# Half of the attention heads scored with keys on partitions, in a two-layer hybrid decoder trunk

## The chip, the cores and the metric

The kernel runs on one core of one Trainium2 chip. A core has five engines that work side by side, each through its own instructions in order: TensorE (PE, matrix products into PSUM; its weight loads are listed as PEld), VectorE (DVE), ScalarE (ACT), GpSimd (POOL) and SyncE (SP, here the queue of the loads). The metric is the device time of one execution in microseconds (us); less is better.

## The reference, cut to what matters

Two layers work on 256 positions of width 1024. Each has a feed-forward part, a mixer and a second feed-forward part. With 256 positions and key blocks of 256 there is one block, so the attention of the mixer is plain causal attention of 8 heads of 64:

```python
def hybrid_layer(x, ...):
    x = x + 0.5 * swiglu(rms_norm(x, ffn1_norm), ffn1_w_gate_up, ffn1_w_down)
    h = rms_norm(x, mix_norm)
    z = h @ w_in                       # u, q, k, v and the gates' inputs gl
    y_pool = multiscale_pool(u, pool_w, pool_scale)
    q = rope(rms_norm(q per head, q_norm)); k = rope(rms_norm(k per head, k_norm))
    # per head: s = q k^T / 8, masked where key > query; p = softmax(s); y = p v
    y_attn = moba_attention(q, k, v)
    gates = sigmoid(gl + b_gate)
    merged = gates[0] * (y_pool @ w_branch_pool) + gates[1] * (y_attn @ w_branch_attn)
    x = x + merged @ w_out
    x = x + 0.5 * swiglu(rms_norm(x, ffn2_norm), ffn2_w_gate_up, ffn2_w_down)
    return x
```

Everything is float32 in and out.

## The kernel before

**Layout.** Activations are held transposed: features on the 128 partitions, the 256 positions in the free dimension. Each float32 operand of a large product is split into two parts (`hi` and `lo`, type fp32r), and a product is three partial products: hi times hi, hi times lo, lo times hi. `chain` (through `prod`, line 118) does the first two in one matmul of 512 columns and the third in one of 256.

**Weights.** They arrive in units of 128 x 2048 values, each loaded by SP into one of 4 `raw` buffers and split in halves: ACT rounds a half to `hi` (line 103), DVE subtracts to get `lo` (line 104). There are 6 buffers `hl` for split halves, so a half can be split as soon as PE has finished with the one six halves earlier. `ask` keeps two units ahead.

**Order.** PE's order is the order in which the program is written. Those of DVE and ACT are laid down at build time by a scheduling planner, which goes by the program's order and by its own estimates of durations; on the chip each engine then keeps to that fixed order, and an instruction that waits holds up everything behind it on its engine. `tc.issue_after` pins a few instructions behind others.

**The mixer**, one call of `mix` per layer, in PE's order: the products `tokens` for q, k and v (positions on partitions), the product for u, the transposes of q and k to features on partitions (`to_features`, line 437), `gate(0)`, scores of heads 0 to 3, gates 1 and 2, transposes of their probabilities (`by_key`, line 472), gate 3, their values (line 481), then scores of heads 4 to 7 (line 446), gates 4 and 5, the pool map, gate 6, `by_key` for heads 4 to 7, gate 7, their values; then the two branch products with `pk` and `yk`, merged with the gates, and the product with `w_out`. A pair `p` is heads 2p and 2p + 1.

**Softmax before.** `scores` puts queries on partitions and keys in the free dimension. `softmax` adds the mask and takes the largest score of each row in one DVE instruction (line 457), ACT takes the exponential with the row's sum as a by-product (line 462), with the norm factor `fq` of the query as its per-partition scale; DVE divides (lines 464 and 466). `by_key` then transposes three 128 x 128 blocks of probabilities per head on PE into PSUM and ACT copies them out (line 474), since the product with v needs the keys on partitions. `halves` splits the result into `yk` (lines 179 and 180).

**PSUM.** The pool `pmm` has two buffers of two banks (gates, k, u, branches), the pool `pat` four buffers of one bank. A gate product needs the `pmm` buffer of the gate before the last one; `drain` (lines 175 and 176) empties it with an ACT copy and a DVE addition. The branch products use the same two buffers and the merge (lines 605 to 614) empties them.

**GpSimd** does small copies inside `pool` (line 500) and, in `reduced` (line 243), one sum over partitions of a 128 x 256 tile ahead of most of the norms.

Of the kernel before, what the change touches and what calls it, by code (L numbers as in the profile page):

```python
# [11 lines left out]
F32 = mybir.dt.float32  # L12
F32R = mybir.dt.float32r
AF = mybir.ActivationFunctionType
OP = mybir.AluOpType
# [3 lines left out]
P = 128  # L19
D = 1024  # L20
S = 256
# [4 lines left out]
NH = 8  # L26
DH = 64
GW = 512
# [4 lines left out]
NEG = -1e30  # L33
# [7 lines left out]
def trunk_kernel(ctx: ExitStack, tc: tile.TileContext, x_in, w_in, pw_in, qkn_in, rope_in, mask_in, band_in, out):  # L41
    nc = tc.nc
    ctx.enter_context(nc.allow_low_precision("float32r parts of exactly split float32 operands"))
    const = ctx.enter_context(tc.tile_pool(name="const", bufs=1))
    raws = ctx.enter_context(tc.tile_pool(name="raws", bufs=4))
    parts = ctx.enter_context(tc.tile_pool(name="parts", bufs=6))
    acts = ctx.enter_context(tc.tile_pool(name="acts", bufs=1))
    tmp = ctx.enter_context(tc.tile_pool(name="tmp", bufs=2))
    small = ctx.enter_context(tc.tile_pool(name="small", bufs=4))
    pmm = ctx.enter_context(tc.tile_pool(name="pmm", bufs=2, space=PSUM))  # L50
    pat = ctx.enter_context(tc.tile_pool(name="pat", bufs=4, space=PSUM))
# [3 lines left out]
    act = nc.scalar.activation  # L55
    tt = nc.vector.tensor_tensor
    stt = nc.vector.scalar_tensor_tensor
    mm = nc.tensor.matmul
# [119 lines left out]
    def halves(d, v):  # L178
        act(d[:, 0, :], v, AF.Copy)  # L179
        tt(d[:, 1, :], v, d[:, 0, :].bitcast(F32), op=OP.subtract)  # L180
# [15 lines left out]
    make_identity(nc, ident)  # L196
    mask = const.tile([P, 3, P], F32, name="mask")
    nc.gpsimd.memset(mask[:, 0, :], 0.0)
    rope = const.tile([P, 2, 2, DH], F32, name="rope")
    cnt = const.tile([P, 16], F32, name="cnt")  # L200

# [2 lines left out]
    acc = acts.tile([P, S], F32, name="acc")  # L204
# [18 lines left out]
    def rsqrt(r, ss, inv):  # L223

        n = r.shape[-1]
        act(r, ss, AF.Abs_reciprocal_sqrt, scale=inv, bias=eps)
        h = small.tile([P, n], F32, name="h", tag="nh" if n == S else f"nh{n}", bufs=1)
        nc.vector.tensor_scalar(h, ss, inv, EPS, op0=OP.mult, op1=OP.add)
        a = small.tile([P, n], F32, name="a", tag="nt" if n == S else f"nt{n}", bufs=1)
        stt(a, r, -0.5, r, op0=OP.mult, op1=OP.mult)  # L230
        tt(a, a, h, op=OP.mult)
        stt(r, a, 1.5, r, op0=OP.add, op1=OP.mult)
# [7 lines left out]
    def reduced():  # L240

        st = small.tile([P, 2, S], F32, name="sa", tag="dr", bufs=1)[:, 0, :]
        nc.gpsimd.partition_all_reduce(st, acc, P, ReduceOp.add)
        return st

    def spread(ah, st):
        for j in range(2):
            prod(st, one_r, ah[:, j, :], j == 0, j == 1)
# [139 lines left out]
    def head_norm(z, rt, c):  # L388

        ms = small.tile([P, 2, NH], F32, name="ms", tag="ms", bufs=2)  # L390
        for t in range(2):
            sq = tmp.tile([P, NH, DH], F32, name="sq", tag="t512", bufs=5)
            act(sq, z[:, t, :], AF.Square)
            nc.vector.tensor_reduce(ms[:, 1 - t, :], sq, axis=AX.X, op=OP.add)
        for t in range(2):
            rc = rt[:, t:t + 1]
            nc.vector.tensor_scalar(ms[:, 1 - t, :], ms[:, 1 - t, :], rc, rc, op0=OP.mult, op1=OP.mult)
        ri = small.tile([P, 2, NH], F32, name="ri", tag="ri", bufs=4)
        rsqrt(ri.rearrange("p t h -> p (t h)"), ms.rearrange("p t h -> p (t h)"), 1.0 / DH)
        for t in range(2):  # L400
            nc.vector.tensor_scalar(ri[:, 1 - t, :], ri[:, 1 - t, :], rt[:, t:t + 1], c, op0=OP.mult, op1=OP.mult)
        return ri
# [27 lines left out]
            tt(zt, zt, ca[:, t, :].unsqueeze(1).to_broadcast([P, NH, DH]), op=OP.mult)  # L430
            tt(zt, zt, sw, op=OP.add)

    def to_features(z, zT):
        for t in range(2):
            ps = pat.tile([P, NH // 2, P], F32, name="tp", tag="at")
            for p in range(NH // 2):
                nc.tensor.transpose(ps[:, p, :], z[:, t, p * P:(p + 1) * P], ident)  # L437
            act(zT[:, :, t * P:(t + 1) * P], ps, AF.Copy)

    def scores(qT, kT, p, fq, scs=None):  # L440

        scs = scs or [pat.tile([P, 3 * P], F32, name="sc", tag="at") for _ in range(2)]
        for c, qs, ks in ((slice(0, S), slice(P, S), slice(0, S)), (slice(S, 3 * P), slice(0, P), slice(0, P))):
            for s, sc in enumerate(scs):
                hs = slice(s * DH, (s + 1) * DH)
                mm(sc[:, c], lhsT=qT[hs, p, qs], rhs=kT[hs, p, ks], start=True, stop=True)  # L446
        return [softmax(sc, fq[:, :, 2 * p + s]) for s, sc in enumerate(scs)]

    def softmax(sc, f):

        nb = small.tile([P, 2], F32, name="nb", tag="nb")
        su = small.tile([P, 2], F32, name="su", tag="su")
        cols = (slice(0, S), slice(S, 3 * P))
        mk3 = mask.rearrange("p a b -> p (a b)")
        for j in range(2):

            nc.vector.tensor_tensor_reduce(sc[:, cols[j]], sc[:, cols[j]], mk3[:, cols[j]], 1.0, 4 * NEG,
                                           op0=OP.add, op1=OP.max, accum_out=nb[:, j:j + 1])
        stt(nb, nb, -1.0, f, op0=OP.mult, op1=OP.mult)
        pr = tmp.tile([P, 3 * P], F32, name="pr", tag="t512", bufs=5)  # L460
        for j in range(2):
            act(pr[:, cols[j]], sc[:, cols[j]], AF.Exp, scale=f[:, j:j + 1], bias=nb[:, j:j + 1],
                accum_out=su[:, j:j + 1])
        nc.vector.reciprocal(su, su)
        for j in range(2):
            di = nc.vector.tensor_scalar(pr[:, cols[j]], pr[:, cols[j]], su[:, j:j + 1], None, op0=OP.mult)
        return pr, di.ins

    def by_key(pr):
        pt = pat.tile([P, 3, P], F32, name="pt", tag="at")  # L470
        for o, c in enumerate((2, 0, 1)):
            nc.tensor.transpose(pt[:, o, :], pr[:, c * P:(c + 1) * P], ident)  # L472
        pT = tmp.tile([P, 3 * P], F32, name="pT", tag="t512", bufs=5)
        act(pT, pt, AF.Copy)
        return pT

    def values(pTs, v, p, y):
        for t in range(2):
            for s, pT in enumerate(pTs):
                h = 2 * p + s  # L480
                mm(y[s * DH:(s + 1) * DH, t * P:], lhsT=v[:, t, h * DH:(h + 1) * DH],  # L481
                   rhs=pT[:, :S] if t == 0 else pT[:, S:], start=t == 0, stop=t == 1)

    def pool_weights(l):
        raw = raws.tile([P, 2 * HALF], F32, name="raw", tag="raw")
        hl = parts.tile([P, 2, HALF], F32R, name="hl", tag="hl")
        nc.sync.dma_start(raw[:, :GW], pw_in[l])
        split(raw[:, :GW], hl[:, 0, :GW], hl[:, 1, :GW])
        return [hl]
# [30 lines left out]
    def mix(l, after, cs):  # L520
        ax = acts.tile([P, 16, 2, S], F32R, name="ax", tag="ga")
        mk, yk, pk, d = ([ax[:, i] for i in range(a, b)] for a, b in ((0, 8), (8, 12), (12, 16), (0, 4)))
        qk = acts.tile([P, 12, S], F32, name="qk", tag="gb")
        qT, kT, u = (qk[:, 4 * i:4 * i + 4, :] for i in range(3))
        gates = acts.tile([P, NK, 2, S], F32, name="gates", tag="gates")

        def big():
            return [pmm.tile([P, 2, 2, S], F32, name="pt", tag="mm") for _ in range(2)]

        def little():  # L530
            return [pat.tile([P, 2, S], F32, name="pl", tag="at") for _ in range(4)]

        def gate(f):
            return pair(unit(), gates[:, f])

        def heads_end(ps):

            y = pat.tile([P, len(ps), S], F32, name="y", tag="at")
            for i, p in enumerate(ps):
                values(pTs.pop(p), v, p, y[:, i, :])  # L540
            for i, p in enumerate(ps):
                halves(yk[p], y[:, i, :])

        ps = little()
        st = reduced()
# [2 lines left out]
        rt = by_token(r)  # L548
        q = joined(ps, "q")
        fq = head_norm(q, rt, DH ** -0.5)  # L550
        ps = big()
        tokens(ps)
        rotate(q, cs[0])
        k = joined(ps, "k")
        ps = little()
        tokens(ps)
        v = joined(ps, "v", rt)
        ask(2)
        rotate(k, cs[1], head_norm(k, rt, 1.0))
        ps = big()  # L560
        for kh in range(2):
            hl = unit()
            for kk in range(4):
                i = kh * 4 + kk
                for g in range(4):
                    chain(ps[g // 2][:, g % 2], hl, kk * 4 + g, hk[i], i == 0, i == NK - 1)
        for g in (0, 2):
            z = u[:, g:g + 2]
            drain(z, ps[g // 2])
            tt(z, z, bc2(r), op=OP.mult)  # L570
        prs, pTs = {}, {}
        to_features(q, qT)
        to_features(k, kT)
        gate(0)
        for p in (0, 1):
            prs[p] = scores(qT, kT, p, fq)
# [6 lines left out]
        gate(3)  # L583
        heads_end((0, 1))

        sc = pmm.tile([P, 3 * P], F32, name="sc", tag="mm")
        prs[2] = scores(qT, kT, 2, fq, [sc, pat.tile([P, 3 * P], F32, name="sc", tag="at")])
        prs[3] = scores(qT, kT, 3, fq)
        pw = pool_weights(l)
        gate(4)  # L590
        gate(5)
        pool_map(pw, d, pk, l)
        gate(6)
        for p in (2, 3):
            pTs[p] = [by_key(pr) for pr, _ in prs[p]]
        gate_act, gate_dve = gate(7)
        for p in (2, 3):
            heads_end((p,))

        def merge(f, ps):  # L600

# [34 lines left out]
        for f in range(4, NK):  # L636
            if f % 2 == 0:
                hl = unit()
            ps = pat.tile([P, 2, S], F32, name="ps", tag="at")
# [148 lines left out]
```

## Time and profile before

| | |
|---|---|
| median of the runs shown | 1001.1 us (1000.55 to 1001.76, three runs) |
| the profiled execution's own time | 1003.4 us |
| its span, first to last instruction | 1001.3 us |
| PE busy | 995.8 us, 99% |
| DVE busy | 797.9 us, 80% |
| ACT busy | 634.4 us, 63% |
| POOL busy | 17.9 us, 2% |
| TensorE's granted clock | 1.000 |

How to read the profile: times are in us from the start of the span. "L457" is line 457 of the kernel. A group of instructions is given as line, engine, operation, output and inputs by the program's names, shapes, count, then busy time in us and mean ns of one, then the engine's idle time just before them and what ended it. Instructions of an engine overlap a little, so their durations add up to somewhat more than the busy time. In the chain of waits a row is start, length, engine and line. In a table of stretches the columns after the length are the busy times of PE, PEld, DVE, ACT and POOL.

### The profile page before, as it was taken

The page shows a single profiled execution, that of the slowest core. Times are in us where ns is not written, and L with a number is a line of the kernel's source. Part 1 is how long each engine was busy: PE and PEld are TensorE (multiplying, and loading weights), DVE is VectorE, ACT ScalarE, POOL GpSimd, SP SyncE. Part 2 cuts the span into 40 slices and gives each one's busy share as a digit, 9 for nine tenths or more (in the row PEclk, how much of TensorE's full clock was granted, in tenths as well). Part 3 has the DMA queues.
Part 4 walks back from the last instruction along what each step waited for, and adds up shares of the span by engine and source line. Part 5 has one row for each costly group of instructions (what it writes and reads, how often), then busy time and mean ns, then how long its engine had stood idle before and what let it go on. Part 6 is the DMA issues. An engine that isn't in the chain of part 4 may idle for free.

```text
span 1001.3 us, 15710 instructions
## 1 busy us (share of the span) xinstructions
PE 995.8 (99%) x6148; PEld 896.5 (90%) x6148; DVE 797.9 (80%) x1313; ACT 634.4 (63%) x1013; POOL 17.9 (2%) x40
## 2 busy tenths in 40 slices
PE   9999999999999999999999999999999999999998
PEld 8888888889899889988889988888889988888897
DVE  7887777798978987776787777778987899888752
ACT  7866655657776766665576666556676777666541
POOL 0000000001000100000000000000000001000000
PEclk9999999999999999999999999999999999999999
DMA  8765655554545665655555565564536456655640
GB/s 301 267 233 192 212 207 193 175 179 138 215 164 174 210 215 200 211 184 200 206 184 200 206 201 184 205 210 169 180 114 228 165 199 210 206 189 207 211 147 22
DMA packets 30601, 192.94 MB, mean 193 GB/s; under 512 B 3392, under 2 KB 5824, under 8 KB 8000
## 3 DMA queue, kind: packets, MB, share of 16 engines
q1 hardware_dynamic: 30240, 191.69, 55.3%
q8 instruction: 48, 0.79, 0.3%
q10 hardware_dynamic: 288, 0.26, 0.1%
q14 instruction: 25, 0.20, 0.1%
HBM read 190.89 MB, written 1.05 MB: 192 GB/s over the span
## 4 chain that ended last, share of the span: by engine, by line
PE 96%; DMA 2%; DVE 1%; ACT 1%; issue 0%; SPq 0%; DVEq 0%
PE ps L118 76%; PE pt L118 9%; PE pl L118 6%; DMA raw<-w 2%; PE pe L118 2%; PE sc L446 1%; PE y L481 1%; DVE hl L104 1%; PE pt L472 1%; PE tp L437 0%; ACT hl L103 0%; PE yp L118 0%; SPq L650 0%; DVE ab L309 0%; DVE ab L176 0%
## 5 line engine op out<-in xcount | busy, mean ns | idle before, releaser
L118 PE MATMUL ps<-hx,hl 128*128 128x512 f32 (+1 forms) x3200 | 541.3, 329 | 1.0 <-DVE ab L176 1.0
L118 PEld LDWEIGHTS ps<-hx,hl 128*128 128x128 f32 x3200 | 481.2, 188 | 56.0 <-DVE ab L176 1.3
L104 DVE TENSOR_TENSOR hl<-raw,hl 128x1024 fp32r<-128x1024 f32 (+2 forms) x371 | 441.9, 1196 | 111.6 <-ACT hl L103 110.8
L103 ACT ACTIVATE hl<-raw 128x1024 fp32r<-128x1024 f32 (+2 forms) x371 | 382.5, 1034 | 132.4 <-PE ps L118 90.0
L118 PE MATMUL ps<-ga,hl 128*128 128x512 f32 (+1 forms) x1024 | 176.3, 328 | 0.0
L118 PEld LDWEIGHTS ps<-ga,hl 128*128 128x128 f32 x1024 | 153.8, 188 | 17.3
L175 ACT ACTIVATE ab<-ps 128x512 f32<-128x512 f32 x84 | 50.2, 598 | 85.9 <-PE ps L118 85.9
L176 DVE TENSOR_TENSOR ab<-ps,ab 128x512 f32<-128x512 f32 x84 | 58.0, 690 | 42.6 <-ACT ab L175 42.5
L118 PE MATMUL ps<-gb,hl 128*128 128x256 f32 (+1 forms) x390 | 69.4, 326 | 0.0
L118 PEld LDWEIGHTS ps<-gb,hl 128*128 128x128 f32 x390 | 58.0, 188 | 6.3
L311 ACT ACTIVATE sg<-ab 128x256 f32<-128x256 f32 x88 | 36.7, 419 | 34.5 <-DVE ab L309 20.9
L118 PE MATMUL pt<-ax,hl 128*128 128x256 f32 x384 | 44.5, 276 | 0.0
L118 PEld LDWEIGHTS pt<-ax,hl 128*128 128x128 f32 x384 | 44.2, 188 | 0.3 <-DVE gates L176 0.3
L118 PE MATMUL pl<-hl,hx 128*128 128x512 f32 (+1 forms) x256 | 44.1, 330 | 0.0
L118 PEld LDWEIGHTS pl<-hl,hx 128*128 128x128 f32 x256 | 38.5, 187 | 5.0
L312 DVE TENSOR_TENSOR sg<-sg,ab 128x256 f32<-128x256 f32 x88 | 36.5, 419 | 0.5 <-ACT sg L311 0.5
L343 ACT ACTIVATE t<-ps 128x256 f32<-128x256 f32 x40 | 15.2, 379 | 32.7 <-PE ps L118 32.7
L208 ACT ACTIVATE hx<-gx 128x256 fp32r<-128x256 f32 x48 | 23.9, 504 | 10.2 <-DVE gx L351 5.3
L309 DVE TENSOR_TENSOR ab<-ab,r 128x256 f32<-128x256 f32 x66 | 27.7, 423 | 1.8
L179 ACT ACTIVATE ga<-sg 128x256 fp32r<-128x256 f32 x64 | 25.6, 404 | 4.1 <-DVE sg L312 3.9
L180 DVE TENSOR_TENSOR ga<-sg,ga 128x256 fp32r<-128x256 f32 x64 | 26.5, 419 | 0.0
L209 DVE SCALAR_TENSOR_TENSOR hx<-gx,hx 128x256 fp32r<-128x256 f32 x48 | 22.8, 480 | 2.8 <-ACT hx L208 2.8
(126 smaller groups left out, 676.3 us busy)
## 6 DMA issues: line engine op xcount, KB each, us to landing
raw<-w SPq DMA_DIRECT2D x176, 1024.0 KB, 4.9
raw<-w SPq DMA_DIRECT2D x9, 256.0 KB, 5.1
raw<-w SPq DMA_DIRECT2D x2, 512.0 KB, 7.3
out_dram<-gx SPq DMA_DIRECT2D x8, 128.0 KB, 1.9
gx<-x SPq DMA_DIRECT2D x3, 256.0 KB, 4.8
raw<-w SPq DMA_DIRECT2D x4, 128.0 KB, 4.7
raw<-pw SPq DMA_DIRECT2D x2, 256.0 KB, 2.7
raw<-w ACTq DMA_DIRECT2D x2, 128.0 KB, 3.8
```

The costliest lines, as they stand in the source:

```text
L103: a = act(hi, w, AF.Copy)
L104: last_split[:] = [a.ins, tt(lo, w, hi.bitcast(F32), op=OP.subtract).ins]
L118: return mm(steps(ps), lhsT=w, rhs=steps(xk), start=first, stop=last)
L175: a = act(t, ps[:, :, 1, :], AF.Copy)
L176: return a.ins, tt(t, ps[:, :, 0, :], t, op=OP.add).ins
L179: act(d[:, 0, :], v, AF.Copy)
L180: tt(d[:, 1, :], v, d[:, 0, :].bitcast(F32), op=OP.subtract)
L208: act(hx[:, f, 0, :], x[:, f, :], AF.Copy, scale=g)
L209: stt(hx[:, f, 1, :], x[:, f, :], g, hx[:, f, 0, :].bitcast(F32), op0=OP.mult, op1=OP.subtract)
L309: tt(ab[:, 0, :], ab[:, 0, :], r, op=OP.mult)
L311: act(sg, ab[:, 0, :], AF.Silu)
L312: tt(sg, sg, ab[:, 1, :], op=OP.mult)
```

## The change

It concerns heads 4 to 7 (pairs 2 and 3) in each layer. Step by step:

- `fq` is multiplied into their part of q before the rotation, since queries no longer lie on partitions at the exponential.
- `to_features` lays q down with its two halves of positions swapped, so that the queries wanted together are adjacent; `scores` of heads 0 to 3 reads the swapped places.
- `scores_by_key` has keys on partitions and queries in the free dimension. A head's scores are three blocks of 128 columns: late keys with late queries, early keys with late queries, early keys with early queries.
- `exps` brings them to SBUF (an ACT copy for the unmasked block, a DVE addition of the triangle `tri` for the two others), takes the maximum of the two late blocks, has GpSimd take the largest over the partitions (`over`), subtracts, takes the exponential without a by-product, and has GpSimd take the sum over the partitions. `inverse` gathers the sums of the two heads into the partitions of their values and takes the reciprocal.
- `values_by_key` multiplies v with the exponentials directly, and the quotient is applied to the result (`yn`) before `halves`. `by_key` isn't called for these heads.
- The scores of pair 2 take one whole buffer of `pmm`; those of pair 3 take two of `pat`.

```diff
+    tri = const.tile([P, 1, P], F32, name="tri")
+    nc.gpsimd.affine_select(tri[:, 0, :], mask[:, 0, :], [[1, P]], OP.is_ge, NEG, base=0, channel_multiplier=-1)
...
-        nc.gpsimd.partition_all_reduce(st, acc, P, ReduceOp.add)
+        over(st, acc, ReduceOp.add)
         return st
+
+    def over(o, z, op):
+        nc.gpsimd.partition_all_reduce(o, z, P, op)
...
-    def to_features(z, zT):
+    def to_features(z, zT, swap=False):
...
-            act(zT[:, :, t * P:(t + 1) * P], ps, AF.Copy)
+            o = (1 - t if swap else t) * P
+            act(zT[:, :, o:o + P], ps, AF.Copy)
...
+    def scores_by_key(qT, kT, p, sc):
+        scs = [z.rearrange("p b c -> p (b c)") for z in sc]
+        for c, ks in ((slice(0, P), slice(P, S)), (slice(P, 3 * P), slice(0, P))):
+            for s, sc in enumerate(scs):
+                hs = slice(s * DH, (s + 1) * DH)
+                mm(sc[:, c], lhsT=kT[hs, p, ks], rhs=qT[hs, p, :c.stop - c.start], start=True, stop=True)
+
+    def exps(scs):
+        e = acts.tile([P, 2, 4, P], F32, name="e", tag="tok", bufs=3)
+        m = tmp.tile([P, 2, 2, P], F32, name="m", tag="t512", bufs=5)
+        for s, sc in enumerate(scs):
+            es = e if len(scs) == 1 else e[:, s:s + 1]
+            n = es.shape[1]
+            act(es[:, :, 1, :], sc[:, :, 1, :], AF.Copy)
+            tt(es[:, :, 0:3:2, :], sc[:, :, 0:3:2, :], tri.unsqueeze(1).to_broadcast([P, n, 2, P]), op=OP.add)
+        tt(e[:, :, 3, :], e[:, :, 0, :], e[:, :, 1, :], op=OP.max)
+        over(m, e[:, :, 2:, :], ReduceOp.max)
+        tt(e[:, :, :2, :], e[:, :, :2, :], m[:, :, 1:, :].to_broadcast([P, 2, 2, P]), op=OP.subtract)
+        tt(e[:, :, 2, :], e[:, :, 2, :], m[:, :, 0, :], op=OP.subtract)
+        act(e[:, :, :3, :], e[:, :, :3, :], AF.Exp)
+        tt(e[:, :, 3, :], e[:, :, 0, :], e[:, :, 1, :], op=OP.add)
+        z = tmp.tile([P, 2, 2, P], F32, name="z", tag="t512", bufs=5)
+        over(z, e[:, :, 2:, :], ReduceOp.add)
+        return e, inverse(z)
+
+    def inverse(z):
+        i = tmp.tile([P, 2, 2, P], F32, name="i", tag="t512", bufs=5)
+        i = i.rearrange("p a t c -> p (a t c)")
+        zc, zi = i[:, :S], i[:, S:]
+        for s in range(2):
+            hs = slice(s * DH, (s + 1) * DH)
+            act(zc[hs], z[hs, s].rearrange("p t c -> p (t c)"), AF.Copy)
+        nc.vector.reciprocal(zi, zc)
+        return zi
...
+    def values_by_key(e, z, v, p, yk):
+        y = pat.tile([P, 2, P], F32, name="y", tag="at")
+        f = y.rearrange("p t c -> p (t c)")
+        for t in range(2):
+            for s in range(2):
+                h = 2 * p + s
+                mm(f[s * DH:(s + 1) * DH, :S if t == 0 else P], lhsT=v[:, t, h * DH:(h + 1) * DH],
+                   rhs=e[:, s, 0, :] if t else e[:, s, 1:3, :], start=t == 0, stop=t == 1)
+        yn = small.tile([P, 2, P], F32, name="yn", tag="sg", bufs=2)
+        for t in range(2):
+            tt(yn[:, t, :], y[:, 1 - t, :], z[:, t * P:(t + 1) * P], op=OP.mult)
+        halves(yk, yn.rearrange("p t c -> p (t c)"))
...
         fq = head_norm(q, rt, DH ** -0.5)
+        for t in range(2):
+            zt = q[:, t, GW // 2:].rearrange("p (h d) -> p h d", d=DH)
+            tt(zt, zt, fq[:, 1 - t, NH // 2:].unsqueeze(2).to_broadcast([P, NH // 2, DH]), op=OP.mult)
...
-        sc = pmm.tile([P, 3 * P], F32, name="sc", tag="mm")
-        prs[2] = scores(qT, kT, 2, fq, [sc, pat.tile([P, 3 * P], F32, name="sc", tag="at")])
-        prs[3] = scores(qT, kT, 3, fq)
+        sc2 = pmm.tile([P, 2, 4, P], F32, name="sc", tag="mm")
+        sc3 = [pat.tile([P, 4, P], F32, name="sc", tag="at")[:, :3, :] for _ in range(2)]
+        for p, sc in ((2, [sc2[:, s, :3, :] for s in range(2)]), (3, sc3)):
+            scores_by_key(qT, kT, p, sc)
+        ez = [exps([sc2[:, :, :3, :]]), exps([z.unsqueeze(1) for z in sc3])]
         pw = pool_weights(l)
...
         gate(6)
-        for p in (2, 3):
-            pTs[p] = [by_key(pr) for pr, _ in prs[p]]
         gate_act, gate_dve = gate(7)
-        for p in (2, 3):
-            heads_end((p,))
+        for p, (e, z) in zip((2, 3), ez):
+            values_by_key(e, z, v, p, yk[p])
```

More of the change, by code (lines that the diff above doesn't have):

```diff
@@ L437, in to_features, with scores @@
                 nc.tensor.transpose(ps[:, p, :], z[:, t, p * P:(p + 1) * P], ident)
-            act(zT[:, :, t * P:(t + 1) * P], ps, AF.Copy)
-    def scores(qT, kT, p, fq, scs=None):
-        scs = scs or [pat.tile([P, 3 * P], F32, name="sc", tag="at") for _ in range(2)]
-        for c, qs, ks in ((slice(0, S), slice(P, S), slice(0, S)), (slice(S, 3 * P), slice(0, P), slice(0, P))):
+            o = (1 - t if swap else t) * P
+            act(zT[:, :, o:o + P], ps, AF.Copy)
+    def scores(qT, kT, p, fq):
+        scs = [pat.tile([P, 3 * P], F32, name="sc", tag="at") for _ in range(2)]
+        for c, qs, ks in ((slice(0, S), slice(0, P), slice(0, S)), (slice(S, 3 * P), slice(P, S), slice(0, P))):
             for s, sc in enumerate(scs):
@@ L571, in mix @@
         prs, pTs = {}, {}
-        to_features(q, qT)
+        to_features(q, qT, True)
         to_features(k, kT)
```

## The prediction

> **What bounds the kernel now.** I read the busy times first, then who TensorE (PE) waits for, then the chain of waits, then the stretch of the change, engine by engine. All rows are of layer 0 unless said. The busy times, and the longest entry of PE's waits after its warm-up:
>
> ```profile
> PE 995.8 (99%) x6148; PEld 896.5 (90%) x6148; DVE 797.9 (80%) x1313; ACT 634.4 (63%) x1013; POOL 17.9 (2%) x40
> ```
>
> ```profile
> PE ps L118 <- DVE ab L176: 1.0, 1, 1.0
> ```
>
> PE is busy for 995.8 of 1001.3 us and the wait shown is 1.0 us. So PE's own instructions are the time, and an edit elsewhere counts only if it makes PE wait. The chain of waits around the change (start, length, what):
>
> ```profile
> 229.01 1.75 PE tp L437 x16
> ...
> 256.76 1.51 PE sc L446 x16
> 258.27 10.96 PE ps L118 x64
> 269.24 1.38 PE yp L118 x12
> 270.61 5.39 PE ps L118 x32
> 276.00 1.31 PE pt L472 x12
> 277.31 5.36 PE ps L118 x32
> 282.67 1.45 PE y L481 x16
> 284.12 22.20 PE pt L118 x192
> ...
> 770.04 1.31 PE pt L472 x12
> ```
>
> The reader sees no hole: scores of heads 4 to 7, gates 4 and 5, the pool map, gate 6, twelve transposes (L472), gate 7, values (L481), then the branches. Layer 1 has the same twelve transposes at 770.04. How full the other engines are there (length, then PE, PEld, DVE, ACT, POOL busy):
>
> ```profile
> 257.00:284.00 27.00, 27.00 (x184) 23.95 (x180) 20.86 (x52) 18.65 (x39) 0.00 (x0) 1.00 0.64 236
> 284.00:292.40 8.40, 8.40 (x76) 8.35 (x73) 6.37 (x8) 8.07 (x18) 0.00 (x0) 1.00 0.44 147
> ```
>
> VectorE (DVE) has 6.1 us idle of the first 27 and 2.0 of the next 8.4; ScalarE (ACT) has 8.4 and 0.3; GpSimd (POOL) does nothing.
>
> **The change part by part.**
>
> *PE.* Removed: by_key for heads 4 to 7, 12 transposes a layer: 2 x 1.31 = 2.62 us, all on the path. The seams to the gates' matmuls may be worth 0.15 us a layer either way: 2.3 to 2.9. Scores become keys by queries: the same 64-row contractions, the same 8 matmuls of 256 and 128 columns per layer, heads of a pair still alternating; only the order of the widths turns. Values take the same widths. No row has the turned order; the nearest are the scores' 1.51 and the values' 1.45, so I bound it by -0.1 and +0.3 us a layer and take 0.
>
> *DVE, removed* (groups of 258.4 to 265 us, the softmax of heads 4 to 7 in one layer):
>
> ```profile
> L457 DVE CUSTOM_DVE_ANT_0 sc<-sc,mask 128x256 f32<-128x256 f32 (+1 forms) x8 | 2.7, 380 | 0.0
> L466 DVE TENSOR_SCALAR pr<-pr,su 128x256 f32<-128x256 f32 (+1 forms) x8 | 2.2, 316 | 0.1
> L457 DVE DVE_READ_ACCUMULATOR2_ANT nb<- 128x1 f32 x8 | 1.2, 144 | 0.0
> L180 DVE TENSOR_TENSOR ax<-y,ax 128x256 fp32r<-128x256 f32 x2 | 0.8, 422 | 0.0
> L464 DVE RECIPROCAL su<-su 128x2 f32<-128x2 f32 x4 | 0.7, 166 | 0.7 <-ACT pr L462 0.7
> L459 DVE SCALAR_TENSOR_TENSOR nb<-nb,ri 128x2 f32<-128x2 f32 x4 | 0.5, 153 | 0.0
> ```
>
> All but the L180 row go: 2.7 + 2.2 + 1.2 + 0.7 + 0.5 = 7.3 us. Prices for what comes (groups of 266 to 287 us):
>
> ```profile
> L104 DVE TENSOR_TENSOR hl<-raw,hl 128x1024 fp32r<-128x1024 f32 x9 | 10.9, 1220 | 3.0 <-ACT hl L103 3.0
> L176 DVE TENSOR_TENSOR gates<-ps,gates 128x512 f32<-128x512 f32 x4 | 2.8, 690 | 2.3 <-ACT gates L175 2.3
> ```
>
> *DVE, added.* Operations of 512 columns: one mask addition and two subtractions, 3 x 0.69 = 2.1. Of 256: two mask additions, two maxima, two subtractions, two sums, 8 x 0.42 = 3.4. Of 128: the four products behind the values, at most 4 x 0.42 = 1.7. Two reciprocals of 256 columns: no row has one. If a column costs what it does elsewhere, 0.42 each. But the two-column reciprocal takes 166 ns and the two-column product of L459 153, 6.5 ns more per column; with the (690 - 422) / 256 = 1.05 ns of an ordinary column that is 0.15 + 256 x 7.5 ns = 2.1. The 2.1 is nearer, being the same instruction, so 4.2 for two. [...] Sum in the stretch: 2.1 + 3.4 + 1.7 + 4.2 - 7.3 = +4.1 us a layer (+0.7 with cheap reciprocals). Two more products of 256 columns scale q early, 0.84 us, in front of q's rotation and far ahead of PE's transposes at 229.01; what they push back is weight splits, which have buffers in hand. I take 0, between 0 and 0.84.
>
> *ACT* (groups of 260.1 to 264.1 us, then of 275 to 285 us):
>
> ```profile
> L462 ACT ACTIVATE pr<-sc,nb,ri 128x256 f32<-128x256 f32 (+1 forms) x8 | 4.0, 515 | 1.3 <-DVE nb L459 1.3
> L462 ACT ACTIVATION_READ_ACCUMULATOR pr<-sc,nb,ri 128x1 f32 x8 | 1.7, 207 | 0.0
> ```
>
> ```profile
> L474 ACT ACTIVATE pT<-pt 128x384 f32<-128x384 f32 x4 | 1.6, 504 | 0.0
> ...
> L179 ACT ACTIVATE ax<-y 128x256 fp32r<-128x256 f32 x2 | 0.7, 382 | 0.0
> ```
>
> Out: 4.0 + 1.7 + 1.6 = 7.3. In: three score copies and four copies of sums, 7 x 0.38 = 2.7, and two exponentials of 768 columns, 2 x 2 x 0.504 = 2.0. ACT gains 2.6 us a layer.
>
> *POOL.* Four all-reduces of 512 columns a layer, where today's has 256 (first column of numbers: shortest, median, longest ns):
>
> ```profile
> L243 POOL PARTITION_ALL_REDUCE sa<-acc x5: 1794/1812/2694, 189.6 to 828.2; - x5
> L226 ACT ACTIVATE r<-sa,eps x5: 510/511/513, 191.4 to 830.9; 128x256 f32<-128x256 f32 x5
> L228 DVE TENSOR_SCALAR h<-sa x5: 283/294/295, 191.4 to 830.9; 128x256 f32<-128x256 f32 x5
> ```
>
> Between 1.8 (cost fixed) and 2 x 2.69 = 5.4 (twice the longest); I take twice the median, 3.6, since every column is worked on: 14.5 us a layer, in series. Latency by that: scores end at 258.3, pair 2's maximum runs 259.4 to 263.0, pair 3's to 266.6, pair 2's sum to 270.2, pair 3's to 273.9; two copies and a reciprocal end at 276.8. Exponentials are wanted at 282.67 - 1.31 = 281.4 and pair 3's are there at about 269; quotients are wanted at 282.8. Six us to spare; at 5.4 each 1.2 us late, which the 48 pool-branch matmuls ahead of yk (48 x 22.20 / 192 = 5.6 us) still cover. POOL's queue holds nothing else here; one triangle is made at the start, where POOL is idle. No DMA moves.
>
> *The new waits.* DVE and ACT work in order, and stand at a sum of GpSimd today:
>
> ```profile
>   ACT r L226: 9.0, 5
>   DVE h L228: 7.4, 4
> ```
>
> DVE stood 4 times for 7.4 us, nearly a whole reduce each. Behind such a wait queue weight splits (1.22) and gate drains (0.69), and PE waits for those. Two rows give the slack:
>
> ```profile
> 269.90 0.69 DVE L176 TENSOR_TENSOR gates<-ps,gates 128x512 f32<-128x512 f32 x1 [0.59 <-ACT gates L175]
> ```
>
> ```profile
> 293.56 1.22 DVE L611 TENSOR_TENSOR gates<-pt,gates 128x1024 f32<-128x1024 f32 x1
> ```
>
> Gate 5's drain ends at 270.6 and gate 7 wants its PSUM at 276.0: 5.4 us. The first merge product ends at 294.8, and the second four branch tiles want that PSUM at 284.12 + 96 x 22.20 / 192 = 295.2: only 0.4 us. So DVE must have worked off any backlog by about 292. Its room a layer: 6.1 + 2.0 idle, less 1.3 (PE is that much sooner), less 4.1 = 2.7 us (6.1 with cheap reciprocals). Waits: of 14.5 us about half passes under the other pair's arithmetic (9.7 us of added work without the products), and splits and drains in the plan's gaps fill most of the rest; I take 2.5 us open, between 0 and 7. That fits, just. Sum: -2.62 + 0.
>
> **The rivals.**
>
> *The wait eats the gain.* DVE backlog over its room by up to 1.3 us a layer gives PE holes as long as the transposes. For it: the room of 2.7 is an estimate with little over; against it: ACT is eased and both drains and splits run ahead. Time: with one us lost a layer 1001.1 - 2.6 + 2.0 = 1000.5.
>
> *Slower: DVE stands in order behind GpSimd.* Place: subtraction behind the maximum, quotient behind the sum. It decides from 2.7 + 1.3 = 4.0 us of open waits a layer. At the upper bound of 7, PE loses 4.3 - 1.3 = 3.0 a layer: 1007.1; halfway, at 5.5, 1004.1. For it: the rows of L226 and L228; against it: those reduces had a single short dependency and little else ready.
>
> [...] A split started beside a reduce:
>
> ```profile
> 507.49 1.79 POOL L243 PARTITION_ALL_REDUCE sa<-acc  x1 [170.68 <-DVE acc L217]
> ```
>
> ```profile
> 507.52 2.14 DVE L104 TENSOR_TENSOR hl<-raw,hl 128x1024 fp32r<-128x1024 f32 x1
> ```
>
> It took 2.14 against 1.22: 0.92 us lost, half the reduce. If every reduce holds DVE for half its length, 14.5 / 2 = 7.2 us a layer go, 4.5 over the room: 1001.1 + 2 x (4.5 - 1.3) = 1007.5. If it holds DVE throughout, 14.5 go: 1001.1 + 2 x (11.8 - 1.3) = 1022.1. Against it: much of that time DVE would wait for the reduce anyway. [...]
>
> **How the numbers follow.** The profiled execution took 1003.4 us with a span of 1001.3, 2.3 us above the median of the runs, 1001.1; the saving is taken from the median: 1001.1 - 2.6 = 998.5 (from the execution's own, 1000.8). Chances: all of it hidden 0.50 (own range 997.7 to 999.1: 2.9 saved and 0.5 us of scatter below, 2.0 saved above); gain eaten 0.18; order behind GpSimd 0.22; shared port at half 0.08, throughout 0.02. About 0.2%, 2 us, is what a measurement here can tell from no change. So faster 0.50, same 0.18, slower 0.32. The range goes from 997.7 up to 1006.0, which leaves out the ends of the slower cases, some 0.17.
>
> **What the changed profile would show.** Right: no L472 for heads 4 to 7 (24 records left of 48), PE's span shorter by 2.6 us, no PE wait in 257 to 300 us, reduces near 3.6 us. [...] I am wrong if open waits exceed 4 us a layer, or if turned scores cost PE more than 1 us a layer.

## The result, and the profile after

The changed kernel took 1015.37 us in the median of five runs (1008.87 to 1018.11), the kernel before 1001.76 (1000.55 to 1002.58) on the same chip: a ratio of 1.0128, with a 95% interval of 1.0111 to 1.0145. It is 13.6 us slower where 2.6 us less was forecast. The profiled execution shown below took 1014.56 us with a span of 1012.8. Not all of the 13.6 us is in it: two of the five runs had a granted clock of 1.000 and took 1008.87 and 1014.56 us, the three others had 0.995 to 0.998 and took 1015.37 to 1018.11. Half a per cent of the span would be 5 us, by my estimate. Only this kernel and that of experiment 9, the two in which PE has waits of 3.2 us and more, have such runs; all others that count here are at 0.999 or 1.000 where their clock is on record. Why it fell is not shown, since the traces kept of these two are of runs at 1.000. Three executions of the experiments below, at granted clocks of 0.70 to 0.85, took 12 to 36% longer and are left out of all figures; the only trace of experiment 4 is of one of them.

The busy times of the profile after:

```profile
PE 998.8 (99%) x6124; PEld 895.2 (88%) x6124; DVE 809.0 (80%) x1287; ACT 631.6 (62%) x991; POOL 42.5 (4%) x49
```

The 24 transposes are gone (6124 PE instructions for 6148), and still PE is busy 3.0 us longer. So two things must have happened: PE stands somewhere, and some of its other work got dearer. The first shows in what PE waits for (us in total, times, longest):

```profile
PE ps L118 <- DVE gates L176: 8.6, 4, 3.2
...
PE ps L118 <- DVE qk L176: 0.6, 2, 0.3
```

Nothing like the first row stood there before. Line 176 is the drain of a gate's PSUM. On PE's timeline of layer 0 (start, length, and in brackets the idle time before and who ended it) both holes stand in the stretch of the change:

```profile
269.89 5.65 PE L118 MATMUL ps<-hx,hl 128*128 128x512 f32 x32 [1.06 <-DVE gates L176]
278.78 5.65 PE L118 MATMUL ps<-hx,hl 128*128 128x512 f32 x32 [3.24 <-DVE gates L176]
284.37 1.52 PE L537 MATMUL y<-e,v 128*64 128x256 f32 x16
```

Gate 6 starts 1.06 us late because the drain of gate 4 is late, gate 7 3.24 us late because that of gate 5 is; layer 1 has the same pair, 4 waits and 8.6 us in all. The values start in time and take as long as before (1.52 us in the timelines of both kernels). Why the drains are late is read from the other three timelines, GpSimd first:

```profile
258.02 1.79 POOL L251 PARTITION_ALL_REDUCE m<-e  x1 [11.11 <-DVE e L474]
262.46 3.23 POOL L251 PARTITION_ALL_REDUCE z<-e  x1 [2.65 <-DVE e L479]
265.60 1.86 POOL L251 PARTITION_ALL_REDUCE m<-e  x1
271.47 4.06 POOL L251 PARTITION_ALL_REDUCE z<-e  x1 [4.01 <-DVE e L479]
```

ACT's rows around the ends of the two sums, 265.69 and 275.53:

```profile
265.73 0.85 ACT L491 ACTIVATE i<-z 64x256 f32<-64x256 f32 x2 [2.94 <-POOL z L251]
266.60 0.60 ACT L175 ACTIVATE gates<-ps 128x512 f32<-128x512 f32 x1
...
275.56 0.84 ACT L491 ACTIVATE i<-z 64x256 f32<-64x256 f32 x2 [4.42 <-POOL z L251]
276.42 0.60 ACT L175 ACTIVATE gates<-ps 128x512 f32<-128x512 f32 x1
```

And DVE's:

```profile
259.84 0.69 DVE L476 TENSOR_TENSOR e<-e,m 128x512 f32<-128x512 f32 x1 [1.36 <-POOL m L251]
...
262.81 2.97 DVE L104 TENSOR_TENSOR hl<-raw,hl 128x1024 fp32r<-128x1024 f32 x1 [0.52 <-ACT hl L103]
266.60 1.75 DVE L492 RECIPROCAL i<-i 128x256 f32<-128x256 f32 x1 [0.82 <-ACT i L491]
268.28 0.63 DVE L476 TENSOR_TENSOR e<-e,m 128x512 f32<-128x512 f32 x1
...
269.15 0.68 DVE L176 TENSOR_TENSOR gates<-ps,gates 128x512 f32<-128x512 f32 x1
...
271.22 1.22 DVE L104 TENSOR_TENSOR hl<-raw,hl 128x1024 fp32r<-128x1024 f32 x1
276.43 1.75 DVE L492 RECIPROCAL i<-i 128x256 f32<-128x256 f32 x1 [4.00 <-ACT i L491]
278.10 0.63 DVE L176 TENSOR_TENSOR gates<-ps,gates 128x512 f32<-128x512 f32 x1
```

This is the first cause. ACT idles 4.42 us for pair 3's sum, then copies it, and only then comes the first half of gate 5's drain (276.42); DVE idles 4.00 us for that copy, takes the reciprocal, and only then does the second half (278.10). Nobody needs that quotient before 284. In front of gate 4's drain stand pair 2's quotient and, behind it, pair 3's subtractions. GpSimd is in order too: its queue holds pair 2's maximum and sum, then pair 3's maximum and sum, so it stands 2.65 and 4.01 us while the arithmetic between the maximum and the sum of one pair is done. Only a small part of the 4.01 us is the fault of pair 2's quotient: in experiment 3, where the quotient stands elsewhere, the same hole is 3.3 us.

The second cause is seen where nothing was changed. PE's long products as the chain of waits has them (start, length), before:

```profile
59.11 126.59 PE ps L118 x752
185.69 10.88 PE pl L118 x64
...
337.06 166.67 PE ps L118 x1000
513.06 166.67 PE ps L118 x1000
679.73 10.89 PE pl L118 x64
...
831.10 166.75 PE ps L118 x1006
```

and after:

```profile
57.88 125.37 PE ps L118 x752
183.24 10.89 PE pl L118 x64
...
339.06 168.33 PE ps L118 x1000
516.83 168.33 PE ps L118 x1000
685.15 10.85 PE pl L118 x64
...
840.94 168.39 PE ps L118 x1006
```

The 1000 matmuls are 500 pairs, one of 512 and one of 256 columns. A pair takes 166.67 / 500 = 333.3 ns before and 168.33 / 500 = 336.7 ns after: 1.0% more, at a granted clock of 1.00 in both, with no wait of PE in any of these stretches. I call them the narrow and the wide spacing. Both occur in both kernels: the first stretch, 752 matmuls, is wide before (126.59) and narrow after (125.37).

The starts in these rows split the 11.5 us by which the span grew:

| stretch | before | after | difference |
|---|---|---|---|
| up to the first mixer | 185.69 | 183.24 | -2.45 |
| mixer, layer 0 | 151.37 | 155.82 | +4.45 |
| feed-forward parts between | 342.67 | 346.09 | +3.42 |
| mixer, layer 1 | 151.37 | 155.79 | +4.42 |
| last feed-forward part to the end | 170.2 | 171.9 | +1.7 |

So the mixers lose 8.9 us, the untouched feed-forward parts behind them 5.1, and 2.45 come back ahead (1.22 of it narrow spacing). In a mixer's 4.45 us there are 4.3 of waits on the gates' drains and 0.3 on that of qk, less 1.31 for the transposes; the remaining 1.2 is products that take longer. A gate that starts behind a wait, for instance, takes 5.65 us in the chain of waits, where gate 7 took 5.36 before.

### The profile page after: what moved, and what is told of

Its sections match the earlier page's. It is cut to its first block, busy times and chain, and to the rows that moved or that the text cites. A ratio compares the mean times of both kernels' runs of the same rounds, so it can differ in the third digit from the quotient of the medians.

```text
span 1012.8 us, 15608 instructions
## 1 busy us (share of the span) xinstructions
PE 998.8 (99%) x6124; PEld 895.2 (88%) x6124; DVE 809.0 (80%) x1287; ACT 631.6 (62%) x991; POOL 42.5 (4%) x49
## 4 chain that ended last, share of the span: by engine, by line
PE 87%; DVE 8%; POOL 2%; issue 1%; ACT 1%; DMA 1%; POOLq 0%; ACTq 0%; DVEq 0%
PE ps L118 72%; PE pt L118 7%; PE pl L118 6%; DVE hl L104 3%; PE pe L118 2%; POOL z L251 1%; DMA raw<-w 1%; DVE gates L176 1%; DVE gates L559 0%; DVE pr L512 0%; DVE sc L503 0%; POOL m L251 0%; DVE i L492 0%; ACT i L491 0%; DVE ax L180 0%
## 5 line engine op out<-in xcount | busy, mean ns | idle before, releaser
L104 DVE TENSOR_TENSOR hl<-raw,hl 128x1024 fp32r<-128x1024 f32 (+2 forms) x371 | 444.6, 1204 | 102.1 <-ACT hl L103 101.5
L176 DVE TENSOR_TENSOR ab<-ps,ab 128x512 f32<-128x512 f32 x84 | 57.9, 689 | 44.7 <-ACT ab L175 44.6
L251 POOL PARTITION_ALL_REDUCE sa<-acc x5 | 10.8, 2158 | 645.9 <-DVE acc L220 645.9
```

Of the source, the lines that this page charges most:

```text
L104: last_split[:] = [a.ins, tt(lo, w, hi.bitcast(F32), op=OP.subtract).ins]
L176: return a.ins, tt(t, ps[:, :, 0, :], t, op=OP.add).ins
L251: nc.gpsimd.partition_all_reduce(o, z, P, op)
```

## The experiments

**Theories.** W (waits): the standing of ACT and DVE behind GpSimd's sums holds up the gates' drains, and PE loses 4.3 us a layer. Its rival within the mixer (L): DVE simply has too much work, in whatever order. For the feed-forward parts: the wide spacing comes as a consequence of PE's new waits, or it comes with any shift of PE's work, waits or not (M in the expectations; M2 there is that neither counts, but something else in the program). A run is compared with the kernel before on the same chip.

**1. Only the gain: the transposes of heads 4 to 7 removed from the kernel before.**

```diff
-            pTs[p] = [by_key(pr) for pr, _ in prs[p]]
+            pTs[p] = [pr for pr, _ in prs[p]]
```

> The kernel before without the twelve transposes a layer (L472) of heads 4 to 7 and without ACT's copies of them; the values of these heads take the untransposed probabilities, so the result differs. It prices the gain by itself. If the transposes were on PE's path and nothing takes their place, the time falls by 2 x 1.31 = 2.6 us against before. If PE's spacing of the matmuls that follow depends on what stands ahead of them (the changed kernel's ran at 168.3 instead of 166.7 ns from there on), it rises by about 3 us although PE never waits.

1005.35 us, a ratio of 1.0037 (1.0024 to 1.0050): slower, with work taken away and nothing added. (The 168.3 and 166.7 of the expectation are us per 1000 matmuls, not ns.) What PE waits for, and its chain:

```profile
PE ps L118 <- DVE ab L176: 1.2, 2, 1.0
```

```profile
335.79 168.33 PE ps L118 x1000
...
832.17 168.39 PE ps L118 x1006
```

No wait in the mixer of any size, and the stretches behind it wide. So the wide spacing does not need PE's waits: it comes here with the mere absence of twelve transposes a layer and of ACT's copies of them; DVE's instructions and their order are those of the kernel before.

**2. GpSimd out of the softmax, DVE's order kept.**

```diff
-        over(m, e[:, :, 2:, :], ReduceOp.max)
+        act(m, e[:, :, 2:, :], AF.Copy)
...
-        over(z, e[:, :, 2:, :], ReduceOp.add)
+        act(z, e[:, :, 2:, :], AF.Copy)
```

> The changed kernel with its four all-reduces a layer in the softmax replaced by ACT copies of the same tiles (0.6 us each), so maxima and sums over keys are left out; the order of DVE's instructions is unchanged. Theory W (DVE and ACT stand in order behind GpSimd and hold up the drains of gates 4 and 5): PE's waits for L176, 8.6 us, go; 999 to 1000, or 1004 to 1005 if PE keeps the wider spacing. Theory L (DVE has too much to do, the two reciprocals of 1.75 us above all): waits of 4 us or more remain.

1000.34 us, 0.9994 (0.9983 to 1.0005). PE's waits and its chain:

```profile
PE ps L118 <- DVE ab L176: 0.7, 1, 0.7
PE ps L118 <- DVE qk L176: 0.5, 2, 0.3
```

```profile
183.79 10.89 PE pl L118 x64
...
334.47 166.67 PE ps L118 x1000
```

DVE issues the same instructions in the same order as in the changed kernel, reciprocals included, and the 8.6 us on the gates' drains are gone: the mixer takes 334.47 - 183.79 = 150.7 us instead of 155.8. ACT has the eight copies in addition, and one rounding of a weight half per layer changes its place there. So DVE's work alone does not do it; what GpSimd's operations put ahead of it does: their latency (1.79 + 3.23 + 1.86 + 4.06 = 10.9 us of operations in layer 0), and 0.83 us by which a sum was longer beside a split, told further down. (The spacing was narrow here, which accounts for 5.1 us more of the 15, in the feed-forward parts.)

**3. The order alone: the quotients pinned behind the drains of gates 5 and 6.**

```diff
-        return e, inverse(z)
+        return e, z
...
+    def behind(g, z):
+        with tc.issue_after(g[0]), tc.issue_after(g[1]):
+            return inverse(z)
...
-        gate(5)
+        g5 = gate(5)
+        z2 = behind(g5, ez[0][1])
...
-        gate(6)
+        g6 = gate(6)
+        z3 = behind(g6, ez[1][1])
```

> The changed kernel with the copies and reciprocal of pair 2's sums put behind the drain of gate 5 and those of pair 3 behind the drain of gate 6; nothing left out. Theory W: gate 7's wait (3.2 us a layer) goes, gate 6's (1.06) falls to about 0.3, since pair 3's subtraction still stands ahead of gate 4's drain: PE waits 1 us or less in all, 999 to 1000.5, or about 1005 with the wider spacing. Theory L: the same work has to be done in the same time, waits of 4 us or more appear elsewhere (merge product, yk, splits).

1005.78 us, 1.0041 (1.0024 to 1.0057), 9.6 us less than the changed kernel (8.8 by the spans of the two profiled executions, 1004.0 and 1012.8, both at a clock of 1.000). Its waits:

```profile
PE pt L118 <- DVE hl L104: 0.8, 2, 0.4
PE ps L118 <- DVE gates L176: 0.7, 2, 0.3
PE ps L118 <- DVE qk L176: 0.5, 2, 0.3
```

Same work, and sums on GpSimd of the same length (3648 ns in the mean of the four, in the changed kernel and in experiment 6, which is this one with a needless matmul): 7.9 of the 8.6 us go with the places of two quotients a layer in the queues of ACT and DVE. On DVE nothing else moves; on ACT some roundings of weights and copies change places too. Of what is left, the 0.4 us a layer on weight splits (L104) in the branch products looks like the backlog that the prediction feared for 292 us; experiment 11 bears on that. In its profiled execution the spacing was wide in layer 0 and narrow in the last stretch.

**4. Pair 3's subtractions pinned too, behind gate 4's drain** (`exps` is cut behind `over(m, ...)`, its second half issued after `gate(4)`).

> As the run before, and pair 3's subtractions, exponential and sums are put behind the drain of gate 4 as well. Theory W: no PE wait is left in the stretch; 2.6 us under before, 998.5 to 999.5, or 1004 to 1005 with the wider spacing. Theory L: waits of 4 us or more.

1006.70 us, 1.0065 (1.0048 to 1.0082): not better than experiment 3. Experiment 7, which has the same order, shows why.

**5. The spacing alone: one needless matmul of 128 columns at the start of the product with w_out**, whose result the next one overwrites, added to experiment 1.

```diff
         pss = little()
+        mm(pss[0][:, 0, :128], lhsT=blk(us[0], 0, 0), rhs=mk[0][:, 0, :128], start=True, stop=True)
```

> The kernel before without the transposes of heads 4 to 7 (probabilities taken untransposed), plus one needless matmul of 128 columns (about 0.06 us) on PE at the start of the w_out product, overwritten by the next. Without it PE never waited, yet stayed at 336.7 ns per pair of matmuls instead of 333.3 from 258 us to the end. Theory M (the spacing is a phase that is set where a new kind of matmul begins, and a small shift there resets it): 333.3 ns from the w_out product on in both layers, 999 to 1000. Theory M2 (the spacing follows from something else, such as placement or the instructions' number): unchanged, 1005 to 1006.

998.98 us, 0.9977 (0.9969 to 0.9986). The chain:

```profile
184.73 10.88 PE pl L118 x64
...
334.90 166.67 PE ps L118 x1000
...
827.73 166.75 PE ps L118 x1006
```

One matmul added makes the kernel 6.4 us shorter than experiment 1 (1005.35). The stretches behind the mixers are narrow now, as in the kernel before, and the mixer takes 150.17 us for 151.37. This is the price of the transposes with the spacing as it was: 1001.74 (the kernel before on this chip) less 998.98 = 2.8 us, with an interval of 1.4 to 3.1; in the traces the two mixers are 2.4 us shorter, two added matmuls of 0.06 us included.

**6, 7 and 8. The same matmul in experiment 3, in experiment 4, and in the kernel before.**

> The kernel with pair 2's and pair 3's quotients pinned behind the drains of gates 5 and 6, plus the same needless matmul. Nothing left out. Theory M: as without it but at 333.3 ns in both layers: 1001 to 1002 (2.2 us of waits, 2.6 saved). Theory M2: 1005 to 1006.

> Pair 3's subtractions behind gate 4's drain as well, plus the needless matmul. Theory W says that no wait for a drain (L176) is left; theory M 333.3 ns: 1000 to 1001. If it is still at 1006 or above, either waits of another kind stand in PE's list (then W is incomplete) or the spacing is the wide one (then M is wrong).

> The kernel before plus the needless matmul, nothing else. It is at 333.3 ns already from the w_out product on. Theory M: if any shift there redraws the phase it may fall to the wide spacing (1005 to 1007) or stay (1002); theory M2: 1002.

Experiment 3 with it: 1003.9 us, 1.0027 (1.0015 to 1.0038); still wide in layer 0, narrow from the end of layer 1's mixer on. It did not buy what it did in experiment 5. The kernel before with it: 1001.71 us, 1.0002 (0.9993 to 1.0010), narrow as before: the matmul itself is no gain. Experiment 4 with it: 1006.3 us, 1.0053 (1.0033 to 1.0073), and here is why the second pin does not help. PE, then DVE, in layer 0:

```profile
284.81 13.26 PE L118 MATMUL pt<-ax,hl 128*128 128x256 f32 x110 [0.98 <-DVE gates L176]
```

```profile
280.20 1.74 DVE L500 RECIPROCAL i<-i 128x256 f32<-128x256 f32 x1
281.86 2.29 DVE L104 TENSOR_TENSOR hl<-raw,hl 128x1024 fp32r<-128x1024 f32 x2
284.07 0.68 DVE L176 TENSOR_TENSOR gates<-ps,gates 128x512 f32<-128x512 f32 x1
```

The whole sequence of pair 3 has moved back, and now gate 7's drain (284.07) stands behind pair 3's reciprocal and two splits; the branch products that need its PSUM wait. The wait has been moved, not removed.

**9. The same matmul in the changed kernel.**

> The changed kernel plus the needless matmul of 128 columns at the start of the w_out product, nothing else. PE's waits (9.4 us) stay. Theory M: if the shift brings the narrow spacing back, 1009 to 1010 (before, less 2.6, plus 9.4 and some restarts); if in one layer only, 1011 to 1013; theory that the wide spacing is a lasting effect of the long waits on PE: 1015 as without it.

1014.53 us, 1.0119 (1.0101 to 1.0138). Waits and chain of its profiled execution (span 1010.6):

```profile
PE ps L118 <- DVE gates L176: 8.6, 4, 3.3
```

```profile
342.03 166.67 PE ps L118 x1000
...
840.45 166.75 PE ps L118 x1006
```

Here the two causes are seen apart: both layers narrow, and the 8.6 us of waits untouched. But the median hardly moved, and its five runs lie from 1009.57 to 1014.98. The granted clock accounts for part of that: the three longest (1014.53 to 1014.98) had 0.995, the two others, 1009.57 and 1012.40, 1.000. What separates those two is not shown, since only the second has a trace; if it is the spacing, the program alone does not fix it.

**10. A needless matmul of 256 columns instead, in experiment 3.**

> Quotients pinned, with a needless matmul of 256 columns (about 0.12 us) instead of 128. In layer 0 the one of 128 left the wide spacing, in layer 1 the narrow one stood with and without it. Theory M: another shift draws again; narrow in both layers gives 1001 to 1002, wide in layer 0 alone 1004, wide in both 1006.

1006.75 us, 1.0055 (1.0043 to 1.0068), wide in both layers: the last stretch reads

```profile
835.30 168.39 PE ps L118 x1006
```

where experiments 3 and 6 have 166.75. So neither length of the added matmul settles the spacing.

**11. A cheap quotient: experiment 6 with a copy in the place of the reciprocal.**

```diff
-        nc.vector.reciprocal(zi, zc)
+        nc.vector.tensor_copy(zi, zc)
```

> Quotients pinned, needless matmul of 128 columns, and the two reciprocals a layer replaced by copies (0.3 to 0.4 us instead of 1.75), so the division is left out. Theory L for what is left of PE's waits in the pinned kernel (1.7 us on drains, splits and merge in the stretch): DVE has 2.8 us a layer less to do and those waits go; only u's drain (0.6) stays. [...] Time 0.5 to 1.5 us under the pinned kernel with the same spacing.

1001.26 us, 0.9996 (0.9987 to 1.0005), narrow in both layers. Its waits:

```profile
PE ps L118 <- DVE gates L176: 0.8, 2, 0.5
PE ps L118 <- DVE qk L176: 0.5, 2, 0.3
```

With the shorter quotient the waits on splits (L104) are gone; so DVE was over its room there, by about the 0.4 us a layer that PE waited. The 0.8 us on the gates' drains stay, which the expectation had going. Without the waits on splits, and with the better spacing, the kernel is just level with before: its span of 999.9 us is 2.0 above that of experiment 5 (997.9), of which 1.3 are these waits; gate 0, which starts behind one of them, also takes 5.67 us for the 5.40 of experiment 5.

**12. The scaling of q moved from DVE to GpSimd, in experiment 6.**

```diff
-            tt(zt, zt, fq[:, 1 - t, NH // 2:].unsqueeze(2).to_broadcast([P, NH // 2, DH]), op=OP.mult)
+            nc.gpsimd.tensor_tensor(zt, zt, fq[:, 1 - t, NH // 2:].unsqueeze(2).to_broadcast([P, NH // 2, DH]), op=OP.mult)
```

> Quotients pinned, needless matmul of 128 columns, and the early products of q with its norm factor moved from DVE to GpSimd; nothing left out. Theory L: gate 0's wait on u's drain (0.3 us a layer) goes, since 0.84 us of DVE's fullest stretch goes; the time falls by 0.6 us at most at the same spacing. If GpSimd's products are slow (over 1 us each) q's rotation and with it k's come later and the wait grows.

1007.84 us, 1.0061 (1.0048 to 1.0074); the wait on L176 of qk, 0.5 us, stays. The expectation missed, and the run does not settle what makes gate 0 late: the chain of waits has 0.63 us of GpSimd's products in each layer, and DVE stood 1.4 us for them in the two, 0.7 of the 0.84 us a layer that it was spared, so that DVE got hardly any room from the edit. No complete version came out ahead of the kernel before.

## Why the prediction was wrong, point by point

**The gain was right.** 2.62 us (2.3 to 2.9) for the transposes; experiment 5 gives 2.8 by the medians and 2.4 by the traces. Scores and values in the new order cost nothing (values 1.52 us and scores 1.58 in the timelines of both kernels).

**The step that failed: "The new waits".** It says "splits and drains in the plan's gaps fill most of the rest; I take 2.5 us open" and "Six us to spare", and it treats DVE's backlog as one sum to be worked off by 292 us. The lateness was reckoned to the consumer of the quotient, the values. But the one who suffers from a wait is whoever stands behind it. The prediction had the drain's slack, 5.4 us for gate 5, and never placed the quotient against it. In the changed kernel ACT alone stands 4.42 us directly ahead of that drain. Open waits were to be 2.5 us a layer, and the prediction called itself wrong above 4: in the rows above DVE stood 1.36 us for a maximum and 0.82 and 4.00 us for ACT's copies of the sums, 6.2 in all. The latency had a wrong step as well. Pair 3's sum was to end 15.6 us behind the scores (258.3 to 273.9) and ended 19.3 us behind them (256.27 to 275.53), though GpSimd's four operations took 10.9 us instead of 14.5. The prediction had both maxima run ahead of both sums, without a gap; in the kernel's queue each pair's sum stands right behind its maximum, and GpSimd idled 2.65 and 4.01 us for the arithmetic between them and what stood ahead of it. That the place of the quotient costs PE the waits is shown from both sides by experiment 2 (same DVE order, no GpSimd) and experiment 3 (GpSimd, other order).

**The rival that came true** is "DVE stands in order behind GpSimd", at its upper bound: it has PE lose 4.3 us a layer, and PE lost 1.06 + 3.24 = 4.3. The place is the one that it named; that the two figures agree is partly luck, since the rival's 4.3 is 7 us of open waits less 2.7 of room on DVE, and PE's is the lateness of two drains. It gave 1007.1 us, and even the fastest run of the changed kernel took 1008.87. It was given 0.22, on the ground that the small reduces of the norms "had a single short dependency and little else ready"; that argument is about how long a reduce takes, not about what is queued behind it.

**What no case held: the spacing.** "PE's own instructions are the time" was taken to mean that untouched instructions keep their durations. They did not: 5.1 us in feed-forward parts that the change does not touch. Experiments 1 and 5 show that it needs neither the new waits nor the added work. What picks the spacing stays open. In most runs it turns at the start of the product with w_out and then holds for a whole stretch; a matmul of 128 columns there turned it in experiment 5, not in layer 0 of experiment 6. The scatter of the changed kernel's runs (9 us, where the kernel before has 2) is in part the granted clock, 0.995 in its two longest; whether the rest is the spacing is not shown, since just one execution of each has a profile.

**Terms.** Reciprocal of 256 columns: 2.1 us taken, 1.75 measured; the dear end was right. GpSimd: 3.6 us taken for each operation; the groups (count, busy us, mean ns) say

```profile
L251 POOL PARTITION_ALL_REDUCE z<-e x4 | 14.6, 3648 | 13.3 <-DVE e L479 13.3
...
L251 POOL PARTITION_ALL_REDUCE m<-e x4 | 7.3, 1825 | 22.2 <-DVE e L474 22.2
```

so the sums hit it and the maxima cost half. Scaling q was taken as free; PE waits 0.3 us a layer more on the drain of qk (L176). DVE's busy time grew by (809.0 - 797.9) / 2 = 5.5 us a layer, for 4.1 + 0.84 reckoned. ACT's fell by 1.4 us a layer, not 2.6, which I did not take apart.

**The shared port**, as the chances call it, was a rival at half and throughout. No run shows a port; the traces show a split and a sum side by side, one of them longer. The split at 262.81, beside the sum of 3.23 us, took 2.97 us instead of 1.22: 1.75 us lost, about half of the sum, as the one row of before had it (0.92 of 1.79). Had the sum held DVE throughout, this split, which began 0.35 us into the sum, would have ended a full 1.2 us behind the sum's end, at 266.9, not at 265.78. The measurement decides for half. The lengthened split did not make PE wait: the reciprocal behind it waited another 0.82 us for ACT's copies. But in the other direction such a pair has a share in the loss. Pair 3's sum began 0.25 us into a split that had 0.97 us still to run, and took 4.06 us; pair 2's, which began 0.35 us ahead of its split, took 3.23, 0.83 less. ACT waited for the end of that sum and gate 7 for ACT, so I estimate that 0.8 of gate 7's 3.24 us come from it.

## What to carry to other kernels

Price a new wait by what is queued behind the waiting instruction on its engine and by when that is due, not by when the awaited result is due; a result that is needed late should stand late in the queue, and two pins a layer gave back 7.9 us of waits here. Write out the queue of every engine for this, the helper's (here GpSimd's) too, before adding up its latency. When PE is 99% busy, compare the time per matmul of untouched stretches first: here a difference of 1% there was worth 5.1 us, where the change under study was to save 2.6. And after a pin, look who is last now: in experiment 7 the wait turned up again one drain further on, 0.98 us behind gate 7's.

## What the runs showed of the hardware

The same pair of matmuls has two steady spacings, 333.3 and 336.7 ns, at the same granted clock and with no wait shown; a needless matmul of 128 columns moved a kernel from one to the other and from 1005.35 to 998.98 us. A maximum over partitions of 512 columns took GpSimd as long as a sum of 256 (1.8 us, the median), the sum of 512 took 3.2 to 4.1. The 4.06 us one started 0.25 us into a split of DVE that kept its usual 1.22 us: in the three such pairs shown here and in the prediction, the one that began later got longer.
